# Doubling the triangular inverses on the 64 columns that change, in place

## The chip, the core and the metric

One Trainium2 chip, one of its cores. The metric is the device time of the whole program in microseconds; 2866.65 us is the median of three runs of the kernel before. All times below are of this program on this core.

## What is computed

Two transformer blocks, one after the other, on 256 latent tokens of 1024 channels (the first block also carries 256 context tokens). The part that the change touches is the gated delta rule in the second block's mixer: 8 heads, two directions, 256 tokens. Per chunk of L tokens the reference solves a unit lower triangular system:

```python
decay = jnp.exp(jnp.where(tri_incl, g_cum[..., :, None] - g_cum[..., None, :], NEG_INF))
k_beta = k * beta[..., None]
lower = jnp.where(tri_strict, jnp.einsum("bhnid,bhnjd->bhnij", k_beta, k) * decay, 0.0)
lhs = lower + jnp.eye(L, dtype=lower.dtype)
rhs = jnp.concatenate([v * beta[..., None], k_beta * jnp.exp(g_cum)[..., None]], axis=-1)
sol = lax.linalg.triangular_solve(lhs, rhs, left_side=True, lower=True, unit_diagonal=True)
```

The other half of that mixer is an mLSTM with 8 heads of its own; a mixture of experts and the last norm follow.

## The kernel before

The kernel works with chunks of 128 tokens, so that one head has four unit triangular matrices of 128 x 128: two directions d, two token tiles jt (index a = 2 d + jt). `gdn_prep` (L931) builds them, transposed, in the tile Bt, and `inverses` (L958) inverts them by doubling: the inverse of the diagonal blocks of size s gives that of size 2 s. `mixer2` (L1105) drives it in four rounds (its loop over c), two heads to a round. In a round, `inverses` first takes the blocks of size 2 with a mask (XT, L976) and transposes them (pX<-ident, L980; copy X, L982). Then come six levels. At each level and head: pQ = Bt X (L988), four products of 128 x 128 by 128 columns; R = pQ times a mask (L990, on DVE); from the second level on XT = the transpose of X (pXT, L995, copied by ACT at L997); pX = XT R (L1001), whose copy by ACT (L1003) is the new X, in a new tile. At the sixth level the operands are exchanged, pX = R XT, and the copy is the transposed inverse that `gdn_out` (L1007) uses. The masks are bfloat16 tiles of 7 levels x 2 directions x 128 columns, loaded by `levels` (L794) in four DMAs with four casts.

All of this is float32. In a product, the first operand is loaded into the array (LDWEIGHTS, 128 stationary columns here) and the second moves through it. The trace shows each float32 product as two passes: L988 has 8 heads x 4 blocks x 6 levels = 192 products and 384 records.

`inverses` yields after its first step and after each level; between the yields `mixer2` writes other work: dense projections (pg and pr, L169 to L171 and L516 to L518), the next two heads' `gdn_prep` (kk and kq products pkk, decay pbc with DVE scans L905 to L910, exponential L913, POOL select L916), the mLSTM heads (E, L1048; pom, L1052) and the previous round's `gdn_out` (pw, prr, pog). Tile schedules the written program: from it each engine gets one fixed order, in which it waits for semaphores. So a product on PE also waits for all that stands ahead of it there. The PSUM banks of pQ, pXT and pX come from a pool of four; the tiles X, XT and R share seven buffers.

Of the kernel before, what the change touches and what calls it, by code (L numbers as in the profile page):

```python
# [9 lines left out]
F32 = mybir.dt.float32  # L10
# [10 lines left out]
D = 1024  # L21
# [14 lines left out]
class Kernel:  # L36
    def __init__(self, ctx, tc, A, NW=4, NTMP=6):
# [21 lines left out]
        # ones in column s  # L59
# [4 lines left out]
        # picks row 32 g + s into column 2 g + s  # L64
# [6 lines left out]
        # adds the rows 32 g + s into column s  # L71
# [3 lines left out]
    def block(self, n, nch):  # L75
        """Pools of one of the two blocks."""
        st = ExitStack()
        self.act = st.enter_context(self.tc.tile_pool(name=f"act{n}", bufs=nch, reuse_waits="tile"))
        self.bp = st.enter_context(self.tc.tile_pool(name=f"blk{n}", bufs=1, reuse_waits="tile"))
        return st  # L80

    # ---- tiles
# [15 lines left out]
    # ---- small parameters as columns [128, rows]  # L98
# [23 lines left out]
    # ---- weights: raw -> (hi, lo), both exact in float32r  # L122
    def weights(self, src, k0, nk, c0, ncol=256, nsplit=2, half=None):
# [7 lines left out]
        with ExitStack() as order:  # L131
            # the second weights after a norm are not split ahead of it
# [11 lines left out]
    def weights_parts(self, srcs, n):  # L144
        """For several [src, first column] of 8 x 128 rows, 256 columns: their (hi, lo), and functions that load and split the i-th of
        n parts of the rows of each."""
# [26 lines left out]
    # ---- adaLN vectors  # L173
# [10 lines left out]
    def ada(self, cm, wsrc, i, bias, out, streams=(0, 1)):  # L184
        """(A generator; its second step is best taken some time after the first.) out [128, NK, 2] =
        silu(c) @ w[:, i-th D columns] + bias columns, the products on DVE, summed over the partitions on PE."""
# [36 lines left out]
    def ada_quarter(self, cm, ws, q, bias, out):  # L223
        """The channels of the q-th 256 of such a vector, the products on PE, for both streams."""
# [17 lines left out]
    # ---- statistics over the model dimension  # L242
    def square(self, c, s, xt, scales=(None,)):
        """Adds (x * scale)^2 of the chunk c of stream s to the sums of its tokens, for each of scales."""
# [10 lines left out]
    def sums(self, s, i=0):  # L255
        """[128, 256] PSUM (all partitions alike): those sums over the model dimension."""
        pt = self.pa("pst")[:, :S]
        self.nc.tensor.matmul(pt, self.ones, self.sq.pop((s, i)), start=True, stop=True)
        return pt

    def rsqrt_table(self, t):
        """Has the table of rsqrt loaded ahead of its use, once t is there."""
        self.table(AF.Abs_reciprocal_sqrt, t)
# [4 lines left out]
    def rsqrt(self, sums, n, tag="rs", k=1):  # L268
        """rsqrt(sums / n + k eps), k 1, 4 or eps: the engine's estimate with one Newton step."""
# [16 lines left out]
    def modulated(self, x, gs, sh, streams):  # L286
        """(x * rstd * gs + sh) split into hi, lo; gs, sh [128, NK, 2]."""
# [9 lines left out]
    def norm_part(self, U, x, gs, sh, s, r, cs):  # L297
        """The chunks cs of the stream s of it, into U."""
# [13 lines left out]
    def scale_cols(self, g, sc, name):  # L312
        """g * (1 + scale): [128, NK, 2]."""
# [16 lines left out]
    def ffn(self, x, U, w_in, w_out, gate, streams, fill=lambda end=False: None, scales=(None,), fills=(), head=None):  # L330
# [3 lines left out]
        for a in range(0, nchunk, 8):  # L334
            b = min(a + 8, nchunk)
            H = []
            for j in range(a, b, 2):
# [14 lines left out]
                if j == 0 and head is not None:  # L352
                    begin, end = head(U, load, split)
                    wdma = self.wdma
                    # the vectors' products run ahead of the others by a quarter
# [46 lines left out]
    def load_x(self):  # L402
        """The streams as 8 tiles [128 channels, 256 tokens] each; self.r: their rstd."""
# [33 lines left out]
    # ---- attention / Fourier mixer  # L437
    def mixer_consts(self):
        nc = self.nc
        # ones in column h of the h-th block  # L440
# [20 lines left out]
    def gemm_t(self, src, U, nk, c0, nchunk, sl, done, first=False, tail=(), half=None):  # L461
        """done(m, psum) for each 128-column chunk of src[:, c0:], as [columns, tokens] of the slice sl;
        for the last two chunks done(m, psum, part) for each part of tail."""
# [25 lines left out]
    def gemm_rows(self, src, U, c0, ncol, toks, done, first=False):  # L489
        """done(t, c, psum[:, :256]) for each 128 tokens x 256 columns, as [tokens, columns]."""  # L490
# [36 lines left out]
    def attend(self, h, Q, K, V, lam, q0, nkeys, out):  # L527
        """out [128 e, 128 q] <- head h of the queries from q0 on, keys 0..nkeys; Q, K: its hi, lo."""
# [30 lines left out]
    def mixer(self, x, U, l, last, lam_init, gcol, bg, gate, fill=lambda end=False: None):  # L559
        """gcol: subln_g column; bg: b_gate columns [128, 16]; gate: [128, NK, 2]."""  # L560
# [50 lines left out]
        # Fourier mixing  # L611
# [5 lines left out]
        # cosines of the frequencies 0..128, sines of 1..127: the others' are these, the sines negated  # L617
# [19 lines left out]
        def gdone(dst, m0):  # L637
            def done(m, p):
                t = self.ch(name="gate")
                # sigmoid(z) = (tanh(z / 2) + 1) / 2, the half taken with w_o's gate  # L640
# [79 lines left out]
    # ---- second block: mixer  # L720
# [21 lines left out]
    def final_and_mod(self, X, gs, sh):  # L742
        """hi, lo of the modulated norm of rms_norm(X, fg); gs: its gain, times fg."""
        nc = self.nc
        sq = [self.sq.pop((LAT, i)) for i in range(2)]
        # rsqrt(mean(x1^2) + eps) of x1 = X fg rsqrt(mean(X^2) + eps), times the latter:
        # rsqrt(mean((X fg)^2) + eps (mean(X^2) + eps))
# [11 lines left out]
    def final_norm(self, X, fg, sq):  # L759
        """(A generator of two steps.) X <- rms_norm(X, fg), in place; sq: the sums of its squares by partition."""  # L760
# [8 lines left out]
    def block2_consts(self):  # L769
        nc, A = self.nc, self.A  # L770
        c = self.bp
        # the last to be read lie first
        self.OA, self.OB = (c.tile([128, 2, 8, 64], F32, name="O" + n) for n in "AB")
        self.sqn = c.tile([128, 2, 8], F32, name="sqn")
        # strictly later (fwd) and strictly earlier (rev): [j, i]
# [8 lines left out]
        # per gate row: bias, sign, coefficient  # L784
# [9 lines left out]
    def levels(self):  # L794
        nc = self.nc
        self.lvl = self.bp.tile([128, 7, 2, 128], BF16, name="lvl")
        for l in range(0, 7, 2):
            n = min(2, 7 - l)
            t = self.tmp(name="lvlt").rearrange("p (l d c) -> p l d c", l=2, d=2)
            nc.sync.dma_start(t[:, :n], self.A["lvl"][:, l:l + n])  # L800
            nc.vector.tensor_copy(self.lvl[:, l:l + n], t[:, :n])

    def gate_rows(self, U):
        """The gates' projections and what the recurrences need of them."""
# [18 lines left out]
        # softplus(z) = max(z, 0) + log1p(exp(-|z|))  # L823
# [6 lines left out]
        # the rounding of w, over w: its slope does for 1 / w between 1 and 2  # L830
# [7 lines left out]
        # log f and i of the mLSTM: rows 0..7 forward, 32..39 backward  # L838
# [10 lines left out]
        # log f_t + m_(t-1) - m_t  # L849
# [8 lines left out]
        # the rows of the two decays, hi on the partitions 0..63, lo on the others  # L858
# [9 lines left out]
        # columns [128 tokens, tile, row] of beta, i - m, exp(-m)  # L868
# [11 lines left out]
    def conv(self, p, wcols, out):  # L880
        """out = 2 silu(centred conv of p [128 channels, 256]); wcols: 5 columns."""
# [9 lines left out]
        # twice silu(o)  # L891
# [4 lines left out]
    def decay(self, row, src, d, bias):  # L896
        """exp(sum of src over the steps from j to i) (+ bias_j), [j tile, i] packed [128, 512], 0 where i
        comes before j in direction d (the block that is all zero is left out)."""
# [15 lines left out]
        # causal within the diagonal blocks (0 and 3 of four)  # L914
# [5 lines left out]
    def products(self, KT, QT, hp, want):  # L920
        """k k^T and k q^T of the head in rows hp.. of the chunk, [j tile, i] packed [128, 512] (PSUM)."""
# [9 lines left out]
    def gdn_prep(self, h, kT, qT, sp, beta):  # L931
# [9 lines left out]
        for d in range(2):  # L941
# [5 lines left out]
            # diagonal blocks of I + A~ diag(beta), transposed, and the block between the tiles  # L947
# [10 lines left out]
    def inverses(self, Bs):  # L958
        """Transposed inverses of the unit triangular blocks of Bs, doubling the size of the inverted diagonal blocks."""
# [5 lines left out]
        def mask(l, flip):  # L965
            m = self.lvl[:, l] if not flip else self.lvl[:, l, ::-1]
            return m.unsqueeze(2).to_broadcast([128, 2, 2, 128])

        def bank(n):
            return self.pa(n).rearrange("p (a b) -> p a b", b=128)  # L970
        four = lambda a: a.rearrange("p (d j) b -> p d j b", d=2)
        n = range(len(Bs))
        XT, X, R = [None for _ in n], [None for _ in n], [None for _ in n]
        for i in n:
            XT[i] = mk("XT")
            nc.vector.tensor_tensor(four(XT[i]), four(Bs[i]), mask(0, True), op=OP.mult)  # L976
# [7 lines left out]
        for l in range(1, 7):  # L984
            for i in n:
# [934 lines left out]
```

## Time and profile before

| | |
|---|---|
| runs | 2863.99, 2866.95, 2866.65 us; median 2866.65 |
| profiled execution | span 2863.3 us from first to last instruction; no other time is listed for it |
| PE busy in the span | 97% |
| the four rounds of `inverses` | about 2258 to 2483 us |
| after them | head norms and gates, three projections, router, experts to the end |

The profiled span lies 3.35 us below the median of the runs. "PE" is the time in which a matmul is in flight; matmuls overlap, so the duration of one is not what a further one costs. For that the distance between successive starts is read: the time of a row of n passes, less one duration, over n - 1. "PEld" is the load of stationary operands, which overlaps PE. "PEclk" is the granted share of TensorE's clock: 1.00 is 2.4 GHz, 0.50 is 1.2 GHz.

### The profile page before, as it was taken

The page shows a single profiled execution, that of the slowest core. Times are in us where ns is not written, and L with a number is a line of the kernel's source. Part 1 is how long each engine was busy: PE and PEld are TensorE (multiplying, and loading weights), DVE is VectorE, ACT ScalarE, POOL GpSimd, SP SyncE. Part 2 cuts the span into 40 slices and gives each one's busy share as a digit, 9 for nine tenths or more (in the row PEclk, how much of TensorE's full clock was granted, in tenths as well). Part 3 has the DMA queues.
Part 4 walks back from the last instruction along what each step waited for, and adds up shares of the span by engine and source line. Part 5 has one row for each costly group of instructions (what it writes and reads, how often), then busy time and mean ns, then how long its engine had stood idle before and what let it go on. Part 6 is the DMA issues. An engine that isn't in the chain of part 4 may idle for free. (4 is left out here: it accounts for less than half of the span.)

```text
span 2863.3 us, 39743 instructions
## 1 busy us (share of the span) xinstructions
PE 2776.7 (97%) x16186; PEld 2266.0 (79%) x16186; DVE 1726.5 (60%) x2974; ACT 1089.8 (38%) x1994; POOL 28.4 (1%) x97
## 2 busy tenths in 40 slices
PE   8999999999999999999999999999998999999997
PEld 6787789876778777788777899779998898895443
DVE  5855675357558656665464565866567865564332
ACT  4222243335624222242222344555446555543222
POOL 0000000000000000000000000000000100000000
PEclk9999999999999999999999999999999999999999
DMA  7644444131123446436464454234555320159997
GB/s 253 207 146 162 145 146 156 63 105 45 45 89 133 162 147 209 168 126 202 154 215 151 149 172 143 74 104 162 177 175 159 102 74 23 33 192 341 366 366 251
DMA packets 354695, 450.27 MB, mean 157 GB/s; under 512 B 13919, under 2 KB 319945, under 8 KB 354505
## 3 DMA queue, kind: packets, MB, share of 16 engines
q1 hardware_dynamic: 352489, 442.42, 46.8%
q0 software_dynamic: 864, 3.15, 0.3%
q8 instruction: 129, 2.11, 0.3%
q10 hardware_dynamic: 1152, 2.10, 0.2%
q14 instruction: 61, 0.50, 0.1%
HBM read 446.57 MB, written 1.05 MB: 156 GB/s over the span
## 5 line engine op out<-in xcount | busy, mean ns | idle before, releaser
L140 ACT CAST whi<-wraw 128x1024 fp32r<-128x1024 f32 (+2 forms) x476 | 466.1, 1005 | 724.7 <-PE py L170 220.8
L141 DVE TENSOR_TENSOR wlo<-wraw,whi 128x1024 fp32r<-128x1024 f32 (+2 forms) x476 | 548.8, 1168 | 254.2 <-ACT whi L140 251.9
L169 PE MATMUL pab<-uh,whi 128*128 128x512 f32 (+1 forms) x1472 | 527.1, 362 | 8.4 <-ACT uh L307 8.4
L171 PE MATMUL pab<-uh,wlo 128*128 128x512 f32 (+1 forms) x1472 | 528.9, 360 | 0.9 <-DVE wlo L141 0.9
L170 PE MATMUL pab<-ul,whi 128*128 128x512 f32 (+1 forms) x1472 | 529.6, 361 | 0.0
L169 PEld LDWEIGHTS pab<-uh,whi 128*128 128x128 f32 x1472 | 276.9, 190 | 60.5 <-ACT uh L307 9.3
L171 PEld LDWEIGHTS pab<-uh,wlo 128*128 128x128 f32 x1472 | 278.8, 190 | 46.7 <-DVE wlo L141 1.6
L170 PEld LDWEIGHTS pab<-ul,whi 128*128 128x128 f32 x1472 | 279.1, 190 | 44.4 <-DVE ul L308 0.4
L198 DVE SCALAR_TENSOR_TENSOR part<-wada,cm,part 128x1024 f32<-128x1024 f32 x238 | 292.6, 1283 | 19.9 <-DMA wada<-in_ada_w_dram 10.8
L171 PE MATMUL pg<-uh,wlo 128*128 128x256 f32 (+1 forms) x864 | 285.6, 331 | 2.3 <-DVE wlo L141 2.3
L169 PE MATMUL pg<-uh,whi 128*128 128x256 f32 (+1 forms) x864 | 286.2, 332 | 1.5 <-ACT cvo L888 0.9
L170 PE MATMUL pg<-ul,whi 128*128 128x256 f32 (+1 forms) x864 | 285.1, 330 | 0.0
L170 PE MATMUL py<-hl,whi 128*128 128x512 f32 (+1 forms) x740 | 265.1, 358 | 0.1
L169 PE MATMUL py<-hh,whi 128*128 128x512 f32 (+1 forms) x740 | 264.7, 358 | 0.0
L171 PE MATMUL py<-hh,wlo 128*128 128x512 f32 (+1 forms) x740 | 263.7, 357 | 0.0
L169 PEld LDWEIGHTS pg<-uh,whi 128*128 128x128 f32 x864 | 165.6, 192 | 20.4 <-issue 2.8
L171 PEld LDWEIGHTS pg<-uh,wlo 128*128 128x128 f32 x864 | 165.4, 192 | 19.7 <-issue 3.7
L170 PEld LDWEIGHTS pg<-ul,whi 128*128 128x128 f32 x864 | 165.8, 192 | 14.6 <-issue 1.9
L169 PEld LDWEIGHTS py<-hh,whi 128*128 128x128 f32 x740 | 139.0, 188 | 23.8 <-issue 1.2
L170 PEld LDWEIGHTS py<-hl,whi 128*128 128x128 f32 x740 | 139.2, 188 | 22.7 <-DVE hl L380 0.3
L171 PEld LDWEIGHTS py<-hh,wlo 128*128 128x128 f32 x740 | 139.1, 188 | 22.7 <-issue 0.4
L377 DVE TENSOR_TENSOR silu<-silu,pab 128x512 f32<-128x512 f32 (+1 forms) x88 | 54.3, 620 | 144.5 <-PE pab L171 144.3
(494 smaller groups left out, 4233.4 us busy)
## 6 DMA issues: line engine op xcount, KB each, us to landing
wraw<-in_ffn_w_in_dram SPq DMA_DIRECT2D x86, 1024.0 KB
wraw<-in_w_in_dram SPq DMA_DIRECT2D x68, 1024.0 KB
wada<-in_w_mod_dram SPq DMA_DIRECT2D x64, 1024.0 KB
wraw<-in_ffn_w_out_dram SPq DMA_DIRECT2D x32, 1024.0 KB
wm<-in_w_gate_dram SPq DMA_DIRECT2D x61, 512.0 KB
wm<-in_w_up_dram SPq DMA_DIRECT2D x61, 512.0 KB
wm<-in_w_down_dram SPq DMA_DIRECT2D x30, 1024.0 KB
wada<-in_ada_w_dram SPq DMA_DIRECT2D x24, 1024.0 KB
```

The lines of the kernel that those rows point to most:

```text
L140: nc.scalar.copy(hi[:, a:b], raw[:, a:b])
L141: nc.vector.tensor_tensor(lo[:, a:b], raw[:, a:b], f32(hi[:, a:b]), op=OP.subtract)
L169: nc.tensor.matmul(ps, wh, uh, start=first, stop=False)
L170: nc.tensor.matmul(ps, wh, ul, start=False, stop=False)
L171: return nc.tensor.matmul(ps, wl, uh, start=False, stop=last)
L198: nc.vector.scalar_tensor_tensor(p, w[:, k], c, p, op0=OP.mult, op1=OP.add)
L377: nc.vector.tensor_tensor(t[:, sl], t[:, sl], P[2 + i], op=OP.mult)
```

## The change

At level l (s = 2^l) only every second group of s columns of X changes: in direction 0 the groups that are first of a pair, in direction 1 the second ones. The change computes R for those 64 columns alone (pQ with a strided moving operand, mask packed to 64 columns), multiplies XT with these 64, and copies the result into these columns of X, in place, one ACT copy for each direction (L1011) where one copy of all four blocks stood before. At the last level it computes the 64 x 64 corner alone (64 stationary and 64 moving columns, L1017) and copies that into XT. R gets two buffers of its own. The masks are 1024 columns in two DMAs and two casts.

```diff
     def levels(self):
-        self.lvl = self.bp.tile([128, 7, 2, 128], BF16, name="lvl")
-        for l in range(0, 7, 2):
...
+        lvl = self.bp.tile([128, 1024], BF16, name="lvl")
+        for i in range(2):
+            t = self.tmp(name="lvlt")
+            nc.sync.dma_start(t, self.A["lvl"][:, i * T:(i + 1) * T])
+            nc.vector.tensor_copy(lvl[:, i * T:(i + 1) * T], t)
+        self.lvl0 = lvl[:, :256].rearrange("p (d c) -> p d c", d=2)
+        self.lvl = lvl[:, 256:].rearrange("p (l d c) -> p l d c", l=6, d=2)
     def inverses(self, Bs):
...
+        def half(n):
+            return self.pa(n)[:, :256].rearrange("p (a b) -> p a b", b=64)
...
         for l in range(1, 7):
+            s = 1 << l
+            cols = lambda x: x.rearrange("p a (n t c) -> p a n t c", t=2, c=s)
             for i in n:
-                pq = bank("pQ")
+                pq = half("pQ")
                 for a in range(4):
-                    nc.tensor.matmul(pq[:, a], Bs[i][:, a], X[i][:, a], start=True, stop=True)
-                R[i] = mk("R")
-                nc.vector.tensor_tensor(four(R[i]), four(pq), mask(l, False), op=OP.mult)
+                    nc.tensor.matmul(pq[:, a].rearrange("p (n c) -> p n c", c=s), Bs[i][:, a], cols(X[i])[:, a, :, a // 2],
+                                     start=True, stop=True)
+                R[i] = self.bp.tile([128, 4, 64], F32, tag="ivr", name="R", bufs=2)
+                nc.vector.tensor_tensor(four(R[i]), four(pq), self.lvl[:, l - 1].unsqueeze(2).to_broadcast([128, 2, 2, 64]),
+                                        op=OP.mult)
...
             for i in n:
-                p = bank("pX")
-                for a in range(4):
-                    nc.tensor.matmul(p[:, a], *((XT[i][:, a], R[i][:, a]) if l < 6 else (R[i][:, a], XT[i][:, a])), start=True, stop=True)
-                new = mk("X")
-                nc.scalar.copy(new, p)
-                (X if l < 6 else XT)[i] = new
+                p = half("pX")
+                if l < 6:
+                    for a in range(4):
+                        nc.tensor.matmul(p[:, a], XT[i][:, a], R[i][:, a], start=True, stop=True)
+                    for d in range(2):
+                        nc.scalar.copy(cols(X[i])[:, 2 * d:2 * d + 2, :, d],
+                                       p[:, 2 * d:2 * d + 2].rearrange("p a (n c) -> p a n c", c=s))
+                else:
+                    for a in range(4):
+                        r, c = (slice(64 * t, 64 * t + 64) for t in (a // 2, 1 - a // 2))
+                        nc.tensor.matmul(p[r, a], R[i][:, a], XT[i][:, a, c], start=True, stop=True)
+                    for d in range(2):
+                        r, c = (slice(64 * t, 64 * t + 64) for t in (d, 1 - d))
+                        nc.scalar.copy(XT[i][r, 2 * d:2 * d + 2, c], p[r, 2 * d:2 * d + 2])
             yield XT
```

The orders of the engines move with it. First PE at the start of the first round. Before:

```order
11350 L980 MATMUL pX<-ident,XT 128x128 x8
11351 L988 MATMUL pQ<-X,Bt 128x128 x8
11352 L1001 MATMUL pX<-R,XT 128x128 x4
11353 L901 MATMUL pbc<-g_rows,identr 128x256 x2
11354 L169 MATMUL pg<-uh,whi 128x256
```

and now (L983, L993, L1009 and L903 are what L980, L988, L1001 and L901 were):

```order
11350 L983 MATMUL pX<-ident,XT 128x128 x8
11351 L993 MATMUL pQ<-X,Bt 128x64 x4
11352 L903 MATMUL pbc<-g_rows,identr 128x256
11353 L993 MATMUL pQ<-X,Bt 128x64 x4
11354 L903 MATMUL pbc<-g_rows,identr 128x256
11355 L1009 MATMUL pX<-R,XT 128x64 x4
11356 L169 MATMUL pg<-uh,whi 128x256
```

The decay products pbc now stand between the heads' pQ and ahead of the first pX; the same number of passes stands ahead of the first pg.

PE where the third round follows the second (the last level's pX, then the next round's transposes). Before:

```order
11762 L901 MATMUL pbc<-g_rows,identr 128x256
11763 L980 MATMUL pX<-ident,XT 128x128 x8
11764 L988 MATMUL pQ<-X,Bt 128x128
11765 L1052 MATMUL pom<-Vb_17898,E 128x65 x2
11766 L1052 MATMUL pom<-Vb_17899,E 128x65
11767 L901 MATMUL pbc<-g_rows,identr 128x256
11768 L1015 MATMUL pw<-V,X 128x64 x2
```

and now:

```order
11762 L1017 MATMUL pX<-XT,R 64x64 x4
11763 L903 MATMUL pbc<-g_rows,identr 128x256
11764 L1017 MATMUL pX<-XT,R 64x64 x4
11765 L983 MATMUL pX<-ident,XT 128x128 x7
11766 L1068 MATMUL pom<-Vb_17898,E 128x65 x2
11767 L1068 MATMUL pom<-Vb_17899,E 128x65
11768 L903 MATMUL pbc<-g_rows,identr 128x256
```

The mLSTM's pbc moved ahead of the second head's last pX, and its pom ahead of the last transpose.

DVE at the same place. Before:

```order
1872 L990 TENSOR_TENSOR R<-pQ,lvl 128x512
1873 L141 TENSOR_TENSOR wlo<-wraw,whi 128x1024
1874 L976 TENSOR_TENSOR XT<-Bt,lvl 128x512
1875 L905 SCALAR_TENSOR_TENSOR E<-pbc,scanm 128x256
1876 L906 SCALAR_TENSOR_TENSOR E<-pbc,scanm 128x128
1877 L976 TENSOR_TENSOR XT<-Bt,lvl 128x512
```

and now:

```order
1867 L996 TENSOR_TENSOR R<-pQ,lvl 128x256
1868 L141 TENSOR_TENSOR wlo<-wraw,whi 128x1024
1869 L907 SCALAR_TENSOR_TENSOR E<-pbc,scanm 128x256
1870 L908 SCALAR_TENSOR_TENSOR E<-pbc,scanm 128x128
1871 L978 TENSOR_TENSOR XT<-Bt,lvl 128x512 x2
```

Both scans now stand ahead of both heads' masks; before, they stood between them.

## Rows read from the trace of the kernel before

**Rows 1.** The page, first part: busy time of each engine.
```profile
PE 2776.7 (97%) x16186; PEld 2266.0 (79%) x16186; DVE 1726.5 (60%) x2974; ACT 1089.8 (38%) x1994; POOL 28.4 (1%) x97
```

**Rows 2.** Windows, second and third round: length, busy (records) of PE, PEld, DVE, ACT, POOL, PEclk.
```profile
2326.00:2376.00 50.00, 48.68 (x383) 44.79 (x380) 32.11 (x76) 26.36 (x55) 3.79 (x8) 1.00 0.13 41
2376.00:2428.00 52.00, 49.94 (x391) 45.72 (x388) 31.18 (x80) 26.53 (x58) 4.67 (x10) 1.00 0.06 20
```

**Rows 3.** Groups on PE, 2258 to 2484 us: records | busy, mean ns | idle before.
```profile
L988 PE MATMUL pQ<-X,Bt 128*128 128x128 f32 x384 | 52.3, 283 | 1.8 <-ACT X L1003 1.2 <-ACT X L982 0.6
L1001 PE MATMUL pX<-R,XT 128*128 128x128 f32 x320 | 42.5, 280 | 1.5 <-ACT XT L997 1.4
...
L1001 PE MATMUL pX<-XT,R 128*128 128x128 f32 x64 | 8.4, 282 | 0.5 <-ACT XT L997 0.5
...
L980 PE MATMUL pX<-ident,XT 128*128 128x128 f32 x32 | 5.7, 315 | 3.0 <-DVE XT L976 2.9
```

**Rows 4.** PE, order of time: start, length, passes; distance between passes at 512, 2, 64, 128 columns.
```profile
2210.63 1.88 PE L1140 MATMUL pkn<-ksq,blk 128*128 128x512 f32 x4
2212.35 1.87 PE L1145 MATMUL pqn<-blk,qsq 128*128 128x2 f32 x16
...
2332.08 1.23 PE L1032 MATMUL pog<-W,P 128*128 128x64 f32 x10
...
2369.81 1.95 PE L988 MATMUL pQ<-X,Bt 128*128 128x128 f32 x16
```

**Rows 5.** Groups on PEld: loads of 128 and of 64 stationary columns.
```profile
L1446 PEld LDWEIGHTS pgu<-wm,hg 128*64 128x64 f32 x512 | 34.2, 136 | 64.0 <-issue 62.4 <-DMA wm<-in_w_gate_dram 0.9 <-DMA gfin<-in_final_norm_g_dram 0.4
...
L1001 PEld LDWEIGHTS pX<-XT,R 128*128 128x128 f32 x64 | 7.5, 191 | 1.7 <-ACT XT L997 1.7
```

**Rows 6.** Groups on ACT: copies of 512 and of 128 columns out of PSUM.
```profile
L1003 ACT COPY X<-pX 128x512 f32<-128x512 f32 x48 | 28.1, 585 | 27.0 <-PE pX L1001 26.6
...
L557 ACT COPY o<-po 128x128 f32<-128x128 f32 x48 | 12.9, 268 | 42.6 <-PE po L555 42.6
```

**Rows 7.** Groups on DVE: products of two tensors, 512 and 256 columns.
```profile
L990 DVE TENSOR_TENSOR R<-pQ,lvl 128x512 f32<-128x512 f32 x48 | 32.4, 684 | 18.4 <-PE pQ L988 18.1
...
L377 DVE TENSOR_TENSOR silu<-silu,pab 128x256 f32<-128x256 f32 x22 | 9.1, 419 | 22.6 <-PE pab L171 22.5
```

**Rows 8.** Start of the third round: DVE, then PE, in order of time.
```profile
2374.37 0.69 DVE L976 TENSOR_TENSOR XT<-Bt,lvl 128x512 f32<-128x512 f32 x1
2375.83 0.69 DVE L905 TENSOR_TENSOR_SCAN E<-pbc,scanm 128x256 f32<-128x256 f32 x1 [0.77 <-PE pbc L901]
...
2376.76 0.67 DVE L976 TENSOR_TENSOR XT<-Bt,lvl 128x512 f32<-128x512 f32 x1
...
2375.63 0.60 PE L980 MATMUL pX<-ident,XT 128*128 128x128 f32 x4
2377.57 0.63 PE L980 MATMUL pX<-ident,XT 128*128 128x128 f32 x4 [1.33 <-DVE XT L976]
```

**Rows 9.** Windows, the clock ahead of, in and behind the rounds (columns as in rows 2).
```profile
2212.30:2215.90 3.60, 3.60 (x25) 2.44 (x24) 0.00 (x0) 3.57 (x9) 0.26 (x4) 1.00 0.62 220
2215.90:2222.70 6.80, 6.80 (x32) 6.68 (x32) 6.02 (x16) 3.51 (x5) 0.13 (x2) 0.50 0.36 96
...
2256.90:2263.70 6.80, 6.46 (x25) 4.97 (x24) 5.46 (x14) 2.75 (x9) 2.25 (x4) 0.50 0.00 0
2263.70:2270.50 6.80, 6.58 (x56) 6.37 (x56) 6.71 (x19) 2.88 (x8) 1.34 (x4) 1.00 0.01 2
2376.00:2380.00 4.00, 2.67 (x23) 2.35 (x21) 2.61 (x6) 2.20 (x5) 0.41 (x1) 1.00 0.74 248
2380.00:2413.00 33.00, 32.28 (x247) 29.12 (x246) 21.66 (x61) 16.51 (x39) 3.85 (x8) 1.00 0.01 1
...
2485.60:2492.40 6.80, 6.05 (x29) 6.08 (x29) 2.45 (x7) 0.85 (x3) 0.55 (x2) 0.50 0.00 0
```

More of the change, by code (lines that the diff above doesn't have):

```diff
@@ L795, in levels @@
         nc = self.nc
-        self.lvl = self.bp.tile([128, 7, 2, 128], BF16, name="lvl")
-        for l in range(0, 7, 2):
[L798 to L801, printed above, removed]
+        lvl = self.bp.tile([128, 1024], BF16, name="lvl")
[5 more added lines that the diff above has]
+        self.lvl = lvl[:, 256:].rearrange("p (l d c) -> p l d c", l=6, d=2)
     def gate_rows(self, U):
@@ L963, in mk @@
             return self.bp.tile([128, 4, 128], F32, tag="iv", name=n, bufs=7)
-        def mask(l, flip):
-            m = self.lvl[:, l] if not flip else self.lvl[:, l, ::-1]
-            return m.unsqueeze(2).to_broadcast([128, 2, 2, 128])
         def bank(n):
             return self.pa(n).rearrange("p (a b) -> p a b", b=128)
+        def half(n):
+            return self.pa(n)[:, :256].rearrange("p (a b) -> p a b", b=64)
         four = lambda a: a.rearrange("p (d j) b -> p d j b", d=2)
@@ L975, in inverses @@
             XT[i] = mk("XT")
-            nc.vector.tensor_tensor(four(XT[i]), four(Bs[i]), mask(0, True), op=OP.mult)
+            nc.vector.tensor_tensor(four(XT[i]), four(Bs[i]), self.lvl0[:, ::-1].unsqueeze(2).to_broadcast([128, 2, 2, 128]),
+                                    op=OP.mult)
         for i in n:
@@ L984, in inverses @@
         for l in range(1, 7):
+            s = 1 << l
+            cols = lambda x: x.rearrange("p a (n t c) -> p a n t c", t=2, c=s)
             for i in n:
-                pq = bank("pQ")
+                pq = half("pQ")
                 for a in range(4):
-                    nc.tensor.matmul(pq[:, a], Bs[i][:, a], X[i][:, a], start=True, stop=True)
-                R[i] = mk("R")
-                nc.vector.tensor_tensor(four(R[i]), four(pq), mask(l, False), op=OP.mult)
+                    nc.tensor.matmul(pq[:, a].rearrange("p (n c) -> p n c", c=s), Bs[i][:, a], cols(X[i])[:, a, :, a // 2],
+                                     start=True, stop=True)
+                R[i] = self.bp.tile([128, 4, 64], F32, tag="ivr", name="R", bufs=2)
+                nc.vector.tensor_tensor(four(R[i]), four(pq), self.lvl[:, l - 1].unsqueeze(2).to_broadcast([128, 2, 2, 64]),
+                                        op=OP.mult)
             if l > 1:
@@ L1841, in shape_constants2 @@
     gsign[40:48] = gsign[56:64] = -1
+    half = [lvl[:, l, d].reshape(128, -1, 2, 1 << l)[:, :, d].reshape(128, 64) for l in range(1, 7) for d in range(2)]
+    lvl = np.ascontiguousarray(np.concatenate([lvl[:, 0, 0], lvl[:, 0, 1]] + half, 1))
     return dict(scanm=scanm, lvl=lvl, blk=blk, blk2=blk2, selm=selm, gsign=gsign)
```

## The prediction

> **What bounds the kernel.** I read the busy shares first: PE is busy 97% of the span, DVE 60%, ACT 38% [rows 1]. So a cheaper DVE or ACT instruction is worth only what PE waits for it. The windows of single rounds agree: PE is busy 48.68 of 50.00 us and 49.94 of 52.00 us, at full clock, with DVE and ACT far from full [rows 2]. The time of the rounds is thus the number of passes on PE times the distance between them, plus small waits. Those waits stand in the groups [rows 3]: ahead of pQ 1.8 us (1.2 on the X copies), ahead of pX 1.5 and 0.5 (XT copies), ahead of the opening transposes 3.0 (mask on DVE). All of it is 6.8 us in 226.
>
> The next question is what sets the distance, since the change halves the columns of most of the doublings' passes. In order of time on PE [rows 4], sixteen pQ passes of 128 moving columns take 1.95 us; with one duration of 0.283 [rows 3] taken off, (1.95 − 0.283)/15 = 0.111 us. Sixteen passes of 2 columns take 1.87 us: (1.87 − 0.283)/15 = 0.106, or 0.125 with nothing taken off. Ten passes of 64 columns take 1.23 us: by the same two bounds 0.105 to 0.137. Only 512 columns are dearer: pkn starts at 2210.63, its follower at 2212.35, 1.72/4 = 0.43. So 2, 64 and 128 columns cost about the same 0.11 us. All of these passes have 128 stationary columns loaded, and a load of 128 columns takes 191 ns where one of 64 takes 136 [rows 5]. I read this as: between 2 and 128 moving columns the stationary side sets the pace.
>
> **The change, part by part.** The number of products does not change.
>
> pQ and the first five levels' pX: 384 + 320 = 704 records with 64 moving columns in place of 128, stationary operand still 128 x 128. By [rows 4] this is worth 0. Bounds: 0, and half of the 112 ns distance for each, 704 x 0.056 = 39 us (a rival below). The strided moving operand of pQ has no row; bounds 0 and, at the 0.125 us of the widest reading of the 2-column row, 384 x 0.014 = +5. I take 0, for the order of columns read should matter less than their number, which matters nothing.
>
> By the Trainium skill, "TensorE: Matmul & The Clock Gate", section "Back-to-back issue gap", the isolated gap follows the moving columns: 134 cycles at 128, about 60 at 64 or fewer. That is 74 cycles or 31 ns less per pass, some 22 us over 704, an estimate. By that rule the 2-column passes should stand at half the distance of the 128-column ones, and the trace disagrees: 0.106 to 0.125 against 0.111 us [rows 4].
>
> The last level: 64 records whose stationary side also falls to 64 columns. 191 − 136 = 55 ns each [rows 5], 64 x 0.055 = 3.5 us, 0.9 a round; bounds 0 and −3.5. At the ends of rounds 1 and 4 other PE work follows: **−1.8**. At the ends of rounds 2 and 3 the next round's transposes follow, and these wait for the masks on DVE. There, before, PE stood 1.33 us for the second head's mask, because a scan stood ahead of it, waiting for pbc [rows 8]. Now both scans stand ahead of both masks, and pbc ahead of the second head's last pX. The scans take 2375.83 to 2376.76 = 0.93 us, a mask 0.67, so the first transpose comes about 1.60 us after pbc. PE fills 8 x 0.056 = 0.45 of it with the last pX: 1.15 of waiting, plus 0.07 where the second mask (0.67) outlasts the first head's transposes (0.60), plus 0.2 for reactions, as between 2377.43 and 2377.57. That is 1.4 in place of 1.33, with 0.9 saved before it: 0.8 a start, **−1.6** for two (bounds 0, and 2 x (0.9 + 1.33) = −4.5).
>
> The X copies: 585 ns for 512 columns becomes two of about 268 [rows 6]. The first half comes 0.32 us earlier and lets two of four products start; the second waits for the first and comes at about 0.54, still ahead of 0.585, and four passes (4 x 0.111 = 0.44) cover it. Of the 1.2 us that pQ waited for this copy [rows 3] I take off **−0.9**; bounds −1.2 and 0. ACT's own sum hardly moves, 96 x 0.268 = 25.7 against 28.1.
>
> R on half the columns: 684 to about 419 ns [rows 7], 48 x 0.265 = 12.7 us of DVE. PE's waits ahead of pX are on XT, not on R [rows 3], so this is hidden behind products of the other head and the dense work: 0. If that cover is gone, 2.0 us (1.5 + 0.5) is what it can be worth.
>
> Masks: two DMAs and two casts fewer, long before the rounds, on SP's queue and DVE. With PE as the bound 0; at most two DVE instructions of 0.68 [rows 7], −1.4. R's own two buffers: before, R, X and XT shared seven, and no wait of any size for one shows in [rows 3]. R is rewritten only after pX of the same head a level earlier, which X's copy, and so pQ, already waits for: 0.
>
> The clock. It is a term because thinner passes give the array less to do. At 2256.90 the clock is 0.50, just as the first round opens with pQ, and is back in the next row, 2263.70 [rows 9]. With 64 columns I expect it back somewhat later, by up to the length of such a row. 6.8 us at half clock cost up to half of them, if every pass takes twice as long; I take half of that: **+1.7**; bounds 0 and 3.4 (half of 6.8).
>
> Sum: −1.8 − 1.6 − 0.9 + 1.7 = −2.6. The profiled execution has a span of 2863.3; 2860.7 after. The median of the runs, 2866.65, lies 3.35 above that span, so **2864.0 us** by the median.
>
> **Rivals.** *B, the clock falls inside a round (ends slower).* For it: at 2212.30 to 2215.90 PE is busy without a gap, 3.60 of 3.60, at full clock, in passes that are mostly of 2 columns; in the following 6.80, again busy throughout, it is at 0.50 [rows 4, 9]. So a busy PE with thin passes has lost the clock in this very program. Against it: between the doublings stand dense products of 256 columns, and 2376.00 to 2380.00 had PE busy only 2.67 of 4.00 and stayed at 1.00 [rows 9]. The place is a round's start, where waits and thin passes come together. Price: a fall as short as 2485.60 to 2492.40 [rows 9] costs up to 3.4 us (half of 6.8); one that lasts as from 2380.00 to 2413.00 costs up to PE's 32.28 us busy there, when every pass takes twice as long: 2861 + 32 + 3 = about 2896. It decides from one long fall, or two short ones: 2864.0 + 2 x 3.4 = 2871, and a third passes the bound of "slower". The Trainium skill, same page, section "Part 1: The HAM clock gate", has the gate follow how busy PE has been. Taken as occupancy alone, thinner passes without gaps would cost no clock; the fall at 2215.90 without a gap speaks against that reading.
>
> *C, the latency of the doublings paces the rounds.* If what PE waits for is the chain copy, pQ, R, pX, copy, then 0.32 + 0.265 us less per level empties all the waits: 6.8 + 3.5 = 10.3 at most. Some of the mask's wait stays; I take −8: 2855.3, median 2858.6. For it: each of the 6.8 us ends on ACT or DVE. Against it: it is spread thin, and 2.9 of it is on a mask that keeps its size.
>
> *D, moving columns set the distance* (the change's plain sense). 768 x 0.056 = 43 us less: 2823.6. Against it stand the three rows of [rows 4]; for it, that those rows are of other tiles, and that 1.95 exceeds 1.87 by 0.08. The skill's gap rule above would end here, at about half the gain.
>
> *E, it doesn't do what it says:* the order of PE shows 64 moving columns in all of pQ and pX, so I give it nothing.
>
> **How the numbers follow.** 0.2% of 2866.65 is 5.7 us, about what a measurement of this kernel can tell from no change: faster is below 2860.9, slower above 2872.4. Forecast 0.50: by its bounds (−1.8 and −4.5 and −1.2 and −1.4 against +5 and +3.4) it spreads from about 2858 to 2873, mostly within 0.2%; 0.09 of it below, 0.03 above. B 0.25: 0.21 above, 0.04 within. C 0.22: 0.17 below, 0.05 within. D 0.03, below. So faster 0.29, slower 0.24, same 0.47. The range: 2857 takes in C's likely value and leaves out D and the best of C (together 0.08); 2882 takes in the short falls of B and leaves out the long ones, 0.12. Of the forecast and C alone the range would be 2857 to 2870.
>
> **What would show it.** Right: groups of sixteen pQ passes still take about 1.9 us; the last level's pX about 1.0; R near 420 ns and the X copies near 268; waits on X copies below 0.5 us; the clock at 1.00 through all windows from 2326 to 2480, back in the first round some us later than 2263.70; the second and third round 50 and 52 us less about one. Wrong: sixteen pQ passes near 1.0 (D); rounds 2 us or more shorter each with the waits gone (C); a window at 0.50 in rounds two to four (B).

## The result, and the profile after

| | before | changed |
|---|---|---|
| median of the runs | 2866.32 us (2863.99 to 2866.95, 4 runs) | 2887.57 us (2886.50 to 2889.06, 4 runs) |
| ratio | | 1.0075 (95% interval 1.0062 to 1.0088) |
| span of the profiled execution | 2863.3 us | 2884.8 us |

The changed kernel is slower by 21 us, 5.6 us above the range. The windows of the changed kernel show where, with the columns of [rows 2]: length, busy time (records) of PE, PEld, DVE, ACT and POOL, PEclk, DMA share, GB/s.

```profile
2256.70:2270.30 13.60, 13.10 (x56) 11.76 (x55) 10.46 (x29) 4.01 (x11) 2.78 (x5) 0.50 0.00 1
2326.00:2376.10 50.10, 47.53 (x384) 43.37 (x384) 31.12 (x80) 25.38 (x70) 4.32 (x9) 1.00 0.17 52
2376.10:2444.40 68.30, 68.30 (x296) 63.94 (x296) 21.34 (x64) 18.49 (x54) 4.11 (x9) 0.50 0.01 2
2444.40:2484.00 39.60, 37.62 (x315) 34.68 (x314) 20.16 (x60) 19.03 (x51) 2.19 (x5) 1.00 0.05 15
```

The third row is the result. For 68.3 us, through most of the third round, TensorE ran at 1.2 GHz, and PE was busy for all of them. The kernel before had 1.00 from 2263.70 to the end of the rounds [rows 2, 9]. Measured between the starts of the rounds' first transposes, the rounds went so (the last one to the start of its last pX):

| | round 1 | round 2 | round 3 | round 4 |
|---|---|---|---|---|
| before | 66.1 | 49.9 | 52.5 | 53.7 |
| changed | 65.6 | 49.1 | 81.4 | 48.1 |

From round 4's last pX to the end of the span it is 381.4 and 381.3 us. The third round lost 28.8 us, and the other three won 7.

PE of the changed kernel around the fall and around the return, in order of time (start, length, passes, in brackets the idle time before and who ended it):

```profile
2367.72 1.89 PE L993 MATMUL pQ<-X,Bt 128*128 128x64 f32 x16
2369.45 1.04 PE L1002 MATMUL pXT<-ident,X 128*128 128x128 f32 x8
2370.42 1.13 PE L929 MATMUL pkk<-bqk 64*128 64x256 f32 x4
2371.48 0.46 PE L1017 MATMUL pX<-XT,R 128*64 128x64 f32 x8
...
2374.02 1.12 PE L983 MATMUL pX<-ident,XT 128*128 128x128 f32 x7 [1.38 <-DVE XT L978]
2375.26 0.88 PE L1068 MATMUL pom<-Vb,E 128*128 128x65 f32 x6
...
2376.36 0.95 PE L1031 MATMUL pw<-V,XT 128*128 128x64 f32 x4
...
2441.22 0.56 PE L169 MATMUL pg<-uh,whi 128*128 128x256 f32 x1
```

The dense passes of round 2 end where the first row starts, at 2367.7. Then come passes with mostly few moving columns, a wait of 1.38 us for the masks, more such passes, and the clock is gone at 2376.1. The first dense pass (256 columns) of the third round starts at 2441.22, and 3.2 us later the clock is back.

The start of the fourth round must be set beside this. In the same trace the same passes follow each other there in the same order, with the same wait:

```profile
2449.08 1.89 PE L993 MATMUL pQ<-X,Bt 128*128 128x64 f32 x16
...
2453.55 0.46 PE L1017 MATMUL pX<-XT,R 128*64 128x64 f32 x8
2455.39 1.12 PE L983 MATMUL pX<-ident,XT 128*128 128x128 f32 x7 [1.38 <-DVE XT L978]
2456.62 0.88 PE L1068 MATMUL pom<-Vb,E 128*128 128x65 f32 x6
```

Here the clock stayed at 1.00 to the end of the round. So these passes with this wait can be followed by a fall, and need not be. DVE at the third round's start shows what the masks stood behind:

```profile
2372.29 0.69 DVE L907 TENSOR_TENSOR_SCAN E<-pbc,scanm 128x256 f32<-128x256 f32 x1 [0.51 <-PE pbc L903]
2372.90 0.40 DVE L908 TENSOR_TENSOR_SCAN E<-pbc,scanm 128x128 f32<-128x128 f32 x1
2373.21 1.27 DVE L978 TENSOR_TENSOR XT<-Bt,lvl 128x512 f32<-128x512 f32 x2
```

The groups of the rounds, 2256 to 2505 us (records, busy, mean ns, idle before):

```profile
L993 PE MATMUL pQ<-X,Bt 128*128 128x64 f32 x384 | 57.7, 308 | 0.6 <-ACT X L985 0.6
L1009 PE MATMUL pX<-R,XT 128*128 128x64 f32 x320 | 50.0, 314 | 1.0 <-ACT XT L1004 1.0
...
L996 DVE TENSOR_TENSOR R<-pQ,lvl 128x256 f32<-128x256 f32 x48 | 20.1, 421 | 37.0 <-PE pQ L993 37.0
L1011 ACT COPY X<-pX 128x128 f32<-128x128 f32 x80 | 17.6, 271 | 48.2 <-PE pX L1009 48.1
...
L983 PE MATMUL pX<-ident,XT 128*128 128x128 f32 x32 | 6.2, 321 | 3.3 <-DVE XT L978 3.2
```

Against [rows 3, 6, 7]: R fell from 684 to 421 ns, the X copies from 585 to 271, and PE no longer waits for these copies (the 0.6 us left are on the copy of the first step, L985). pQ and pX have grown, as part of them ran at half clock.

### The profile page after: what moved, and what is told of

It is laid out like the page before. It is cut to its first block, busy times and chain, and to the rows that moved or that the text cites. A ratio compares the mean times of both kernels' runs of the same rounds, so it can differ in the third digit from the quotient of the medians.

```text
span 2884.8 us, 39817 instructions
## 1 busy us (share of the span) xinstructions
PE 2800.6 (97%) x16186; PEld 2290.9 (79%) x16186; DVE 1713.7 (59%) x2972; ACT 1084.3 (38%) x2042; POOL 28.3 (1%) x97
```

## The experiments

Theory "thin" puts the fall and its length on the passes with 64 moving columns, theory "wait" on the wait for the masks.

**128 columns again.** In `wide_both` all of the change stays, but pQ and the first five levels' pX stream 128 columns. The 64 added ones are written to PSUM and not used:

```diff
-pq = half("pQ")
+flat = self.pa("pQ")
 for a in range(4):
-    nc.tensor.matmul(pq[:, a]..., Bs[i][:, a], cols(X[i])[:, a, :, a // 2], ...)
+    o = 128 * a - 64 * (a // 2)
+    nc.tensor.matmul(flat[:, o:o + 128].rearrange("p (t n c) -> p n t c", t=2, c=s), Bs[i][:, a], cols(X[i])[:, a], ...)
+pq = flat.rearrange("p (a b) -> p a b", b=128)[:, :, :64]
...
-nc.tensor.matmul(p[:, a], XT[i][:, a], R[i][:, a], ...)
+nc.tensor.matmul(p[:, a].rearrange("p (t c) -> p t c", t=2), XT[i][:, a], R[i][:, a].unsqueeze(1).to_broadcast([128, 2, 64]), ...)
```

> The changed kernel, but every pQ and the first five levels' pX stream 128 moving columns again; the 64 added ones are written to PSUM and read by nobody. R, the copies in place, the masks, the waits and the last level's corner stay as in the change. Theory thin (the 64-column passes make the clock fall at the third round's start, at 2376, and hold it down for 68 us): clock 1.00 from 2280 to 2480, or one short stretch at 0.50, third round about 52 us, median 2858 to 2866. Theory wait (the 1.38 us in which PE waits for the first-step masks in that place is enough, the columns do not matter): the same fall at the third round's start, 60 us or longer, median 2884 to 2890.

Measured: 2860.63 us, ratio 0.9973 (0.9962 to 0.9983). Its windows of rounds two to four:

```profile
2326.00:2376.00 50.00, 48.62 (x388) 43.98 (x387) 29.53 (x78) 24.58 (x67) 4.15 (x9) 1.00 0.10 29
2376.00:2428.00 52.00, 50.75 (x406) 46.26 (x406) 28.72 (x84) 25.30 (x70) 4.61 (x10) 1.00 0.08 26
2428.00:2480.00 52.00, 48.26 (x383) 43.43 (x383) 25.68 (x80) 25.17 (x70) 3.25 (x8) 1.00 0.06 14
```

With the clock at 1.00, 27 us come back although the columns are twice as many. But the order had moved too, and PE's wait ahead of the transposes was gone, so this alone does not acquit the wait.

The two halves of that edit apart:

> The changed kernel with the first five levels' pX at 128 moving columns (64 of them read by nobody) and pQ left at 64. Theory thin: half of the thin passes are gone, so the fall is shorter than 68 us or absent, median 2858 to 2878. Theory wait: unchanged, 2884 to 2890.

Measured: 2863.81 us, 0.9987 (0.9978 to 0.9997), with falls of 3.4 us at 2375.5 and of 13.7 us at 2426.7, both at a wait of 1.38 us for the masks.

> The changed kernel with pQ at 128 moving columns (64 read by nobody) and the first five levels' pX left at 64. Theory thin: as with pX widened alone, the falls inside the rounds add up to some 5 to 25 us at 0.50 in place of 68, median 2860 to 2872. If pX's thin passes alone hold the clock down: 2880 to 2890.

Measured: 2860.40 us, 0.9976 (0.9966 to 0.9985). The profiled execution, with falls of 3.4 us at 2351.7 and of 6.8 us at 2402.9, took 2866.02 us and is the slowest of the ten, so the others may have fewer or shorter ones. Either half keeps the clock's losses short.

**128 columns in the third round alone** (the edit above under a flag, set for c = 2).

> The changed kernel with 128 moving columns (64 read by nobody) in pQ and the first five levels' pX of the third round alone; rounds one, two and four keep 64. Theory thin-holds (the thin passes that follow the fall are what keeps the clock down for 68 us, while the fall itself comes from the waits and thin passes at the seam of rounds two and three): a fall at the third round's start that lasts under 15 us, median 2860 to 2868. Theory thin-triggers (only the thin passes ahead of the seam decide, and a fall once begun takes its time): a fall at 2376 as long as in the changed kernel, 2884 to 2890. Theory third-round-only (the third round's own thin passes do both): no fall in the third round, 2856 to 2862, and a fall in the fourth round is then possible.

Measured: 2859.81 us, 0.9977 (0.9967 to 0.9986). PE's order up to the seam is the changed kernel's, and so is the wait; its windows:

```profile
2326.00:2374.70 48.70, 46.73 (x380) 42.68 (x379) 29.90 (x80) 24.12 (x67) 4.33 (x9) 1.00 0.14 42
2374.70:2378.10 3.40, 3.40 (x18) 3.40 (x18) 1.30 (x4) 1.37 (x3) 0.41 (x1) 0.50 0.14 47
2378.10:2425.00 46.90, 45.88 (x365) 41.41 (x364) 24.80 (x73) 21.88 (x62) 3.81 (x8) 1.00 0.00 1
2425.00:2477.00 52.00, 50.17 (x410) 46.27 (x409) 27.32 (x80) 26.76 (x75) 3.28 (x9) 1.00 0.09 24
```

and PE at its seam:

```profile
2372.76 1.12 PE L983 MATMUL pX<-ident,XT 128*128 128x128 f32 x7 [1.38 <-DVE XT L978]
...
2375.99 2.02 PE L995 MATMUL pQ<-X,Bt 128*128 128x128 f32 x8
```

The fall comes as in the changed kernel, but the clock is back after 3.4 us, 2.1 us after the start of the first 128-column pQ. **The thin passes behind the seam held the clock down for 68 us**; behind the seam this run differs in the third round's columns and, with them, in some of its order. The first round agrees. Around its start every kernel here loses the clock, for 13.7 us in all eight kernels with 64 columns there, and for 6.8 or 10.2 us in the nine with 128 in pQ, in pX or in both.

**The wait taken away.** First, the masks written a round ahead, at the end of `gdn_prep`:

```diff
+xt = self.bp.tile([128, 4, 128], F32, tag="iv", name="XT", bufs=7)
+nc.vector.tensor_tensor(xt..., bt..., self.lvl0[:, ::-1]..., op=OP.mult)
-return P, bt, off
+return P, bt, off, xt
```

> The changed kernel (64 columns everywhere), but the first-step mask is applied at the end of a head's preparation, a round ahead, so that PE finds XT ready when a round starts. Theory wait: PE's 3.3 us ahead of the first transposes go, no fall inside the rounds, median 2852 to 2862. Theory thin: the clock falls in spite of it at some round's start, median 2875 to 2890.

Measured: 2873.23 us, 1.0021 (1.0011 to 1.0030). The wait for masks was gone from rounds two to four, yet the clock fell twice in them:

```profile
2354.60:2368.20 13.60, 12.26 (x58) 12.26 (x59) 4.29 (x11) 4.61 (x12) 1.26 (x3) 0.50 0.01 1
2416.00:2426.30 10.30, 10.30 (x52) 10.30 (x51) 3.11 (x8) 2.84 (x8) 0.50 (x2) 0.50 0.00 0
```

In the new order PE waited 8.2 us for XT copies ahead of pX, 3.62 of them up to 2355.95 and 3.67 up to 2414.83, next to the two falls. So the masks are not the only wait that matters, and neither theory's expectation came true; and with 128 columns in that order no clock was lost in rounds two to four:

> 128 moving columns in pQ and pX, and the first-step mask applied at the end of a head's preparation. Theory thin: with the clock at 1.00 inside the rounds, what is left is the order: the 3 us of waits for masks are gone, but the XT copies were waited for 8.2 us in the run with early masks and 64 columns; median 2855 to 2866, and 7 to 18 us below that run. Theory wait (early masks are slow for their order, not for the clock): within 4 us of that run's 2873.

Measured: 2862.41 us, 0.9987 (0.9977 to 0.9996), 10.8 us below `masks_early`.

Next, masks written ahead of a round's last piece of side work only:

> The changed kernel (64 columns, dense projection where it was) with the first-step masks of the next round written a little earlier, so that at the third round's start both stand ahead of the scans on DVE; PE's order at that seam is as in the changed kernel but for the place of one pom. Theory wait-triggers (1.38 us without work beside thin passes start the fall, thin passes then hold it): PE's wait for the masks is under 0.5 us, no fall at 2376, median 2854 to 2862. Theory thin-triggers (the thin passes at the seam alone start it): a fall at the third round's start as in the changed kernel, 2880 to 2890. Either way, a fall at another seam can come instead and would show in the clock.

Measured: 2888.27 us, 1.0079 (1.0065 to 1.0092). A miss of the edit: the scheduler put the scans first again at the third round's start, PE's order through that round is the changed kernel's, and it waited as there; the clock was at 0.50 from 2378.5 to 2446.8, back 3.0 us after the first dense pass.

```profile
2376.51 1.12 PE L989 MATMUL pX<-ident,XT 128*128 128x128 f32 x7 [1.38 <-DVE XT L964]
```

So the order was tied:

```diff
+first = self.firsts([st[h][1] for h in (2 * c + 2, 2 * c + 3)])
+with self.tc.issue_after(self.lastmask):
+    f()
```

where f is the last mLSTM head of rounds two and three.

> As masks_mid, but the scans of the last mLSTM head of rounds two and three are tied behind the next round's masks on DVE, so that both masks really stand ahead of them at the third and fourth round's start. 64 columns, dense projection where it was. Theory wait-triggers: PE's wait for the masks there is under 0.5 us, no fall at the third round's start, median 2852 to 2862. Theory thin-triggers: the clock falls at the third round's start without the wait and stays down some 60 us, 2880 to 2890; a short fall (under 15 us) would mean that the wait took part.

Measured: 2857.33 us, 0.9967 (0.9954 to 0.9979). PE at the seam, and the windows:

```profile
2370.89 0.46 PE L1024 MATMUL pX<-XT,R 128*64 128x64 f32 x8
...
2371.59 0.46 PE L1024 MATMUL pX<-XT,R 128*64 128x64 f32 x8
2371.98 1.19 PE L990 MATMUL pX<-ident,XT 128*128 128x128 f32 x8
2373.36 2.05 PE L1000 MATMUL pQ<-X,Bt 128*128 128x64 f32 x14 [0.19 <-ACT X L992]
```

```profile
2326.00:2372.00 46.00, 45.21 (x368) 41.66 (x368) 28.55 (x76) 22.79 (x63) 3.82 (x8) 1.00 0.10 30
2372.00:2421.80 49.80, 48.83 (x394) 44.62 (x392) 27.86 (x81) 24.83 (x71) 4.70 (x10) 1.00 0.07 22
2421.80:2470.00 48.20, 46.99 (x385) 43.60 (x382) 24.01 (x73) 23.45 (x66) 2.85 (x7) 1.00 0.07 23
```

All 64 columns, no wait for masks at the seam, no fall. **Without the wait of 1.38 us the fall did not come.** (One more thing moved: pom and pbc now stand behind the first pQ.) The kernel before had such a wait of 1.33 us with 128 columns and kept its clock [rows 8, 9].

That the wait takes part fits all traces: each of the nine falls inside rounds two to four begins during a wait of PE of 0.56 to 3.67 us or within 2.1 us of its end. That it suffices is not so: the changed kernel's own fourth round starts with the same passes and the same wait and keeps its clock. What decides between its third and its fourth round no run here shows.

**Dense passes behind the seam.** The return at 2444.4 came 3.2 us after the first dense pass, so the dense projection (`step`) of rounds two to four was written first in a round's side work:

```diff
-    side += [mlstm(4), mlstm(5), step, mlstm(6), mlstm(7)]
+    side = [step] + side + [mlstm(4), mlstm(5), mlstm(6), mlstm(7)]
 else:
-    side += [mlstm(2 * c - 2), step, mlstm(2 * c - 1)]
+    side = [step] + side + [mlstm(2 * c - 2), mlstm(2 * c - 1)]
```

> The changed kernel (64 columns everywhere) with the dense projection of rounds two, three and four written as the first of a round's side work instead of behind the preparations and mLSTM heads, so that its 256-column passes follow the seam. Theory thin: dense passes behind the seam bring the clock back soon, so the long stretch at 0.50 in the third round is cut to under 20 us, median 2860 to 2878; the ends of the rounds, now without dense work, may show falls of their own. Theory order (the 68 us belong to this round's work whatever stands first): 2882 to 2892.

Measured: 2854.05 us, 0.9952 (0.9935 to 0.9969), no fall in rounds two to four: below the 2860 to 2878 of theory thin. In this order, too, the wait for masks had shrunk (0.3 us in all), so the run does not separate that from the dense passes. Then four kernels with that order on one chip:

> The changed kernel with the dense projection first in rounds two to four, once more, beside the three below on one chip: 2852 to 2857 by both theories.

> The same order of the side work, with 128 moving columns (64 read by nobody) in pQ and the first five levels' pX. Theory load-bound (with the clock held, 64 moving columns save PE nothing, since the 128 stationary columns set the distance): within 4 us of dense_again. Theory thin-pays (64 columns are cheaper once the clock holds): 10 us or more above dense_again.

> The kernel before with the last level's 64x64 corner and the dense projection first; 128 columns, full copies of X and full masks. Theory load-bound, and copies and R of half the size hidden: within 4 us of dense_again. If the shorter copies and R pay in this order: 4 to 10 us above it.

> The kernel before with the dense projection first in rounds two to four and nothing else. If the corner is worth the 5 to 7 us that it gave by itself and the order the rest: 5 to 8 us above corner_dense, so about 2859 to 2864. If the order alone gives the gain: within 2 us of corner_dense. If the order helps thin passes only: 2865 to 2868, as the kernel before.

Measured: 2855.06 (0.9960, 0.9946 to 0.9974), 2862.88 (0.9993, 0.9984 to 1.0002), 2864.12 (0.9993, 0.9984 to 1.0002), 2866.59 (0.9998, 0.9989 to 1.0007). The order does nothing for the kernel before; it helps the thin one. `dense_wide` lies 7.8 us above `dense_again`, between the two expectations. `corner_dense`, which also has the whole copies and the whole R, lies only 1.2 us above `dense_wide`: at 128 columns the halved copies and R are worth little, and the gain comes with the 64 columns. The windows of rounds two and three, `dense_again`:

```profile
2326.00:2371.30 45.30, 44.82 (x368) 41.41 (x367) 27.77 (x68) 23.29 (x64) 3.41 (x7) 1.00 0.20 63
2371.30:2420.30 49.00, 47.88 (x394) 44.53 (x394) 28.43 (x81) 25.59 (x71) 4.58 (x10) 1.00 0.04 12
```

and `dense_wide`:

```profile
2330.00:2377.20 47.20, 46.06 (x369) 41.64 (x368) 27.70 (x70) 23.48 (x63) 3.74 (x8) 1.00 0.19 60
2377.20:2429.50 52.30, 50.02 (x395) 44.66 (x394) 28.16 (x81) 25.04 (x71) 4.66 (x10) 1.00 0.04 11
```

Both are at full clock, with the same work in the third round, and the thin one needs 3.3 us less. The median distance between pQ passes, and between pX passes, is 0.112 us in both, so the usual step is no shorter. In sum over rounds two to four, PE's steps longer than 0.2 us are fewer with 64 columns (none in place of 6 behind pQ passes, 6 in place of 18 behind pX). Of what the third round gains, 3.0 us stand in the steps that lead up to a pQ or a pX pass. That speaks for results that are ready earlier, but the scheduler's order differs as well, and these runs do not part the two.

The two cures together:

> The same early masks together with the dense projection first. No wait at the seams and dense passes behind them: no fall inside rounds two to four, and 0 to 2 us below the 2855 of the dense projection first alone.

Measured: 2851.55 us, 0.9952 (0.9939 to 0.9966), no fall in rounds two to four. This is the lowest median of the study, 14 us below the one before and 36 below the change as made; its ratio is that of `dense_first`, and its four rounds take 209.4 us where those of `dense_again` take 209.5. So beside the dense order the early masks gained nothing in the rounds.

**The corner alone**, on the kernel before:

```diff
+if l == 6:
+    for a in range(4):
+        r, c = (slice(64 * t, 64 * t + 64) for t in (a // 2, 1 - a // 2))
+        nc.tensor.matmul(p[r, a, :64], R[i][:, a, r], XT[i][:, a, c], start=True, stop=True)
+    for d in range(2):
+        r, c = (slice(64 * t, 64 * t + 64) for t in (d, 1 - d))
+        nc.scalar.copy(XT[i][r, 2 * d:2 * d + 2, c], p[r, 2 * d:2 * d + 2, :64])
+    continue
```

> The kernel before with the last level alone changed: its pX computes the 64x64 corner with 64 stationary and 64 moving columns and is copied into XT in place. All else (128 columns, full copies, masks) as before. Both theories: that group of 64 records falls from 8.4 to about 4 us. Thin: no fall inside the rounds, median 2861 to 2866. Wait: less work stands ahead of the masks at the third and fourth round's start, the wait is longer than the 1.33 us of before, and the clock may fall there: 2866 to 2888.

Measured: 2860.98 us, 0.9973 (0.9961 to 0.9984), no fall in rounds two to four. Two groups of its rounds, and one row of PE in order of time:

```profile
L980 PE MATMUL pX<-ident,XT 128*128 128x128 f32 x32 | 5.3, 313 | 0.1
...
L1003 PE MATMUL pX<-XT,R 128*64 128x64 f32 x64 | 3.1, 231 | 0.5 <-ACT XT L997 0.5
```

```profile
2375.22 0.73 PE L1003 MATMUL pX<-XT,R 128*64 128x64 f32 x16
```

The mean distance is (0.73 − 0.231)/15 = 0.033 us against 0.111 at 128 and 128 columns: 64 x 0.078 = 5.0 us, by this estimate the largest part of the 6.7 measured. The wait for masks went from 3.0 [rows 3] to 0.1 us with the order. What the corner gives hangs on the order: with the dense projection first it is 2.5 us (2866.59 − 2864.12), half of the least that was expected there.

## Why the prediction was wrong

**The failed step is the clock: the sum has a term for it at the first round's start alone (+1.7) and nothing for the other rounds, and the chance of rival B, which held the rest, was too small.** B named the place ("a round's start, where waits and thin passes come together") and a price for a long fall of 32 us. The runs showed such a fall: 68.3 us at half clock, with which the third round took 81.4 us against 49.9 in `masks_lead`, 31.5 more. But B had 0.25, of which 0.12 for long falls, and the range left these out. Two arguments against it were wrong:

- "2376.00 to 2380.00 had PE busy only 2.67 of 4.00 and stayed at 1.00." That stretch had 128-column passes around its wait. `wide_third` shows what the columns do to the length of a fall, and `masks_lead` that without the wait none came.
- "Between the doublings stand dense products." For most of the third round none do: the last ones before the seam end at 2367.7, the next start at 2441.22. It was so in the kernel before, where none starts between 2369.69 and 2413.88; its clock held there without them, and so it did in `masks_lead`, with 64 columns and none from 2367.0 to 2410.4. Where the dense work stands within a round was not looked at.

The length of a fall was also misjudged. The prediction treated short and long ones as alike likely; yet what ended the falls here was the work that followed, and thin passes followed for 65 us. The row at 2215.90 [rows 9] had a hint of it: the dense passes start at 2218.28 in it, and the clock was back 4.4 us later. That the fall came in the third round and not also in the fourth, which starts alike, was not foreseen and is not explained.

**Clock, the other term.** The first round got its clock back at 2270.3 in place of 2263.7 [rows 9], as expected "somewhat later"; the round as a whole still went from 66.1 to 65.6 us.

**Moving columns do not set the distance: right; that they are worth nothing: not in every order.** Sixteen pQ passes take 1.89 us at 64 columns and full clock, and 1.95 at 128 [rows 4]. Rival D is out. But `dense_again` is 7.8 us below `dense_wide`, so the term at 0 missed something that comes another way than by the distance. The Trainium skill, "TensorE: Matmul & The Clock Gate", section "Back-to-back issue gap", gives an isolated product 134 cycles at 128 columns and about 60 at 64 or fewer, and says that in a stream of loads and products both set the spacing. The trace, with 0.112 us at either width and 128 stationary columns, agrees with the second and not with the first.

**The last level: direction right, size not.** 3.5 us were forecast from the load's duration, 5.0 come out of the distances in `corner_only`. Where the load fell to 136 from 191 ns, as forecast, the distance fell to 0.033 from 0.111 us, so the load's duration is not what a pass costs.

**The seam: the wait was forecast as 1.4 us and came out at 1.38.** (The 0.2 us for reactions were 0.14 in the row they were read from; 1.36 would have come as close.) What was missed is what it could set off.

**X copies, R, masks: right.** No wait on the X copies is left, R takes 421 ns.

**Rival C came near in number where the clock held, in part by luck.** In `masks_lead` the four rounds took 65.4, 47.7, 49.9 and 49.0 us, 10.3 less than before, as much as C's "10.3 at most", and its 2857.33 us lie near C's 2858.6. Of this, some 5.0 us are the corner's by its distances, and 2.9 the masks' wait, which the later edit took away and not the change. Of the other 3.8 us of C's waits 3.2 are left, 1.1 ahead of pQ and 2.1 ahead of pX. So the rounds did have some 10 us to give, and the change's own part of that was hidden under the fall.

**The forecast's spread** ended at 2873; with its bounds added it ends at 2875 (2866.65 + 5 + 3.4). Either is far below what was measured.

## What to carry to other kernels

Before columns are taken off a product, read from the trace what sets the distance between its passes. If it does not change with the moving columns, as here, fewer of them do not bring the passes closer, and the clock can be lost: the change cost 21 us. Look for places where thin passes and a wait meet without dense work near, and put a dense piece or an early operand there; with that, the same 64 columns were 10 to 14 us below the kernel before. Read the granted clock of every round, too, for a kernel can lose it at one place and keep it at another that looks the same. Shrinking the stationary side as well, as in the corner, brought the passes closer, and was worth 6.7 us alone and 2.5 in another order.

## What the runs showed of the hardware

- TensorE stayed at 1.2 GHz for 68.3 us with PE busy 68.30 of 68.30, mostly in passes of 64 or 65 columns and transposes, with some pbc and pkk passes between. It was back at 2.4 GHz after 3.4 us where 128-column passes took their place (`wide_third`), and in the changed kernel 3.2 us after the start of the first dense pass. The Trainium skill, same page, section "Part 1: The HAM clock gate", says that the gate follows how busy PE has been; if busy means occupied, as the profile counts it, these runs disagree.
- The same passes with the same wait of 1.38 us were followed by that fall in the third round and by none in the fourth (2455.39, 1.00 to the end of the round).
- Passes of 64 moving columns on 64 stationary columns stood 0.033 us apart in the mean (alternately some 0.013 and 0.045), those on 128 stationary columns 0.112: less than a third for half the stationary side.
